# The Fourier branch of a two-layer diffusion trunk: c_x by tokens, the position transform ahead of the channel transform

## The chip, the cores and the metric

The kernel runs on one core of a Trainium2 chip. The metric is the device time of one execution in microseconds; the kernel before takes 1150.8 us (median of 3 runs, 1149.96 to 1150.83). The engines named below are TensorE (PE in the profile, its weight loads PEld), VectorE (DVE), ScalarE (ACT), GpSimd (POOL) and SyncE (SP), which issues most of the DMAs.

## The reference, cut to what matters

Two layers (`DEPTH = 2`) work on 256 latent tokens and 256 context tokens of width 2048. In each layer one projection `h @ w_in` gives the columns of three branches: a gMLP branch (a_u, a_v, a_g), attention (q, k, v, b_g) and the Fourier branch (c_x, c_g), which is

```python
def fourier_mix(xc, w_f, b_f):
    bsz, t, _ = xc.shape
    xg = xc.reshape(bsz, t, C_GROUPS, C_DIM).astype(jnp.float32)
    y = jnp.fft.fft2(xg, axes=(1, 3), norm='ortho').real.astype(xc.dtype)
    y = jnp.einsum('btgc,gcd->btgd', y, w_f) + b_f
    return y.reshape(bsz, t, C_WIDTH)
...
    y_a = chunk_gmlp(jax.nn.gelu(a_u), jax.nn.gelu(a_v), g_sgu, w_s, b_s) * jax.nn.silu(a_g)
    y_b = attn_fn(b_q, b_k, b_v) * jax.nn.silu(b_g)
    y_c = fourier_mix(c_x, w_f, b_f) * jax.nn.silu(c_g)
    return jnp.concatenate([y_a, y_b, y_c], axis=-1)
```

There are four groups of 128 channels; the transform goes over the 256 positions of a stream and the 128 channels of a group, and only its real part is kept. Latent and context tokens are two separate streams. In the last layer only the latent stream needs more than its keys and values. The branches go through an output projection, a norm and a gated residual.

## The kernel before

Matrices are float32 held as two parts, a rounded one and the rest: `split_into` casts on ScalarE (L437) and subtracts on VectorE (L438). A product is three matmuls, `mm3` (L420 to L422), or in layer 1 two, `mm2` (L536, L537), where the rounded and the residual part of the latent activations lie side by side, so that one 512-column and one 256-column matmul do, and `joined` (L542, L543) adds the two halves.

The activations `hh`/`hl` have 16 row tiles (k). Weights come as a stream `W` of halves of 128 x 1024: a DMA into `raw` (3 buffers), the cast `whi` (L398) and the subtraction `wlo` (L400), 4 buffers each, taken by `W.next()` in the order of `units()`. `tunit(n)` computes one head of 128 columns with the weights stationary and the tokens moving: 16 k, 48 matmuls of 512 columns in layer 0; `tunit1` is that of layer 1 with 32 matmuls.

PSUM has two pools: `mm_ps` of six banks and `ms_ps` of two.

TensorE's order is the program's order. Work that depends on other engines is put between its matmuls by `later`: a task is a generator which yields how long its next piece is to lie back, and `later.tick` adds up the time that TensorE was given. VectorE, ScalarE and SP are ordered by a scheduler by priority and readiness.

A layer runs so: a_v and the first a_u heads together (`start_av`, `start_au`; in layer 0 three a_u heads, the third in a bank of the small pool); then the remaining a_u heads (one in layer 0, two in layer 1, phase au); c_x in four units (cx); a_g and c_g in four units each, each with its `gate`; k, v, q, b_g. Tasks:

- `branch_a`: gelus of a_u (L724) and a_v (L726), squares back into the a_v banks (L728), the norm, then four position mixes on TensorE (L736).
- `fourier_mats`: the channel cosine and sine matrices times each group's `w_f` (L751), split into `mg`, `mgl`. It starts 3 us after the phase begins.
- `fourier(g, ps)`, one for each c_x unit as it ends: cosine and sine parts are taken apart by adding and subtracting mirrored positions (L760 to L764), split, multiplied by the folded channel matrices (`ps_f`), split again with a repair of one partition, and after `YF` multiplied by the position matrices `ct` and `nst` (`ps_z`), then copied with the bias (L781).
- in layer 1 `boundary_ctx`, begun by `after_start` at the start of c_x: it closes layer 0 for the context (multiplications, an accumulating DMA from GpSimd, squares), takes a norm (column sums L458 and a broadcast L471 through the small pool) and makes layer 1's context activations (`make_h`, L498 to L507), which the k units read.
- `mods`: the modulation of both layers on VectorE (L204, L206) from 512 KB loads into `mraw`, paced by `W.next()`; in layer 1 the gate (L242, L244) from the k units on.

The constants `ct` and `nst` are loaded as two blocks of 128 x 256 and split. The output rows of the groups lie in `yo[12..15]` in layer 0 and in `kt` buffers in layer 1.

Of the kernel before, what the change touches and what calls it, by code (L numbers as in the profile page):

```python
# [7 lines left out]
F32 = mybir.dt.float32  # L8
F32R = mybir.dt.float32r
BF16 = mybir.dt.bfloat16  # L10
AF = mybir.ActivationFunctionType
ALU = mybir.AluOpType

P = 128
D = 2048
KT = D // P
S = 256
T = 2 * S
# [6 lines left out]
COL = dict(au=0, av=512, ag=1024, q=1536, k=2560, v=2816, bg=3072, cx=4096, cg=4608)  # L25


def units():

    u = []  # L30
    u += [("av", COL["av"], 512, 4 * i, 4) for i in range(4)]
    u += [("au01", COL["au"], 256, 8 * i, 8) for i in range(2)]
    u += [(f"au{h}", COL["au"] + 128 * h, 128, 0, 16) for h in (2, 3)]
    u += [(f"cx{h}", COL["cx"] + 128 * h, 128, 0, 16) for h in range(4)]
    u += [(f"ag{h}", COL["ag"] + 128 * h, 128, 0, 16) for h in range(4)]
    u += [(f"cg{h}", COL["cg"] + 128 * h, 128, 0, 16) for h in range(4)]
    u += [(f"k{h}", COL["k"] + 128 * h, 128, 0, 16) for h in range(2)]
    u += [("v", COL["v"], 256, 8 * i, 8) for i in range(2)]
    u += [(f"q{h}", COL["q"] + 128 * h, 128, 0, 16) for h in range(8)]
    u += [(f"bg{h}", COL["bg"] + 128 * h, 128, 0, 16) for h in range(8)]  # L40
    return u
# [9 lines left out]
COFF, _o = {}, 0  # L51
# [3 lines left out]
NCONST = _o  # L55
# [11 lines left out]
def trunk_kernel(ctx: ExitStack, tc: tile.TileContext, xT, xhalf, cT, wss, wsl, wmod, win, wout0, wout1, const, vec, rows,  # L67
                 wmat, bs, sink, out):
    nc = tc.nc
    V, A, G, PE, DMA = nc.vector, nc.scalar, nc.gpsimd, nc.tensor, nc.sync  # L70
# [6 lines left out]
    def sb(shape, dt, tag, bufs=1):  # L77
        cnt[0] += 1
        return pool.tile(shape, dt, tag=tag, bufs=bufs, name=f"{tag}_{cnt[0]}")

    def w2k(shape, dt=F32):
        return sb(shape, dt, "w2k", W2K)

    def mm_ps(name="mm"):
        cnt[0] += 1
        return psum.tile([P, 512], F32, tag="mm", bufs=6, name=f"ps_{name}_{cnt[0]}")

    def ms_ps(name="ms"):
        cnt[0] += 1
        return psum.tile([P, 512], F32, tag="ms", bufs=2, name=f"ps_{name}_{cnt[0]}")  # L90


    yo = [sb([P, T], F32, f"yo{k}") for k in range(KT)]
    ct = sb([P, KT, 2], F32, "ct")
# [29 lines left out]
    def vc(l, name):  # L124
        o, w = VOFF[name]
        return vecs[:, l, o:o + w]

    identr = sb([P, P], F32R, "identr")
    ident = identr.bitcast(F32)
# [143 lines left out]
    state = {"ctx": [], "phase": "", "owed": 0.0}  # L273
    mods = mod_rest()
    LAG = 400
    YF = [5.0, 2.8], [6.0, 5.2]
    RATE = dict(au0=2, cx0=2.2, ag0=2.2, cg0=2.2, k0=2, v0=2, q0=1.8, bg0=2.2, out0=2.8,
                k1=2.5, v1=2.5, q1=1, bg1=0.3, out1=1.4)
    NEAR = [0] * 14 + [1, 2, 3]
# [46 lines left out]
    later = Later()  # L326
# [90 lines left out]
    W = Stream()  # L417

    def mm3(ps, st, mv, start, stop):
        PE.matmul(ps, st[0], mv[0], start=start, stop=False)  # L420
        PE.matmul(ps, st[0], mv[1], start=False, stop=False)  # L421
        PE.matmul(ps, st[1], mv[0], start=False, stop=stop)  # L422

    def part(w, c):

        def of(t):
            if not isinstance(t, list):
                return t[:, c]
            n = t[0].shape[-1]
            return t[c.start // n][:, c.start % n:c.start % n + c.stop - c.start]  # L430

        return of(w[0]), of(w[1])

    split = {}

    def split_into(hi, lo, src):
        A.copy(hi, src)  # L437
        V.tensor_tensor(out=lo, in0=src, in1=hi.bitcast(F32), op=ALU.subtract)  # L438
        return hi, lo

    def split_of(src, tag):
        n = src.shape[-1]
        return split_into(sb([P, n], F32R, tag + "h"), sb([P, n], F32R, tag + "l"), src)
# [38 lines left out]
    def h_of(l, k, sl):  # L482

        if l == 0:
            return hh[k][:, sl], hl[k][:, sl]
        s, a = sl.start // S, sl.start % S
        t, b = (hh, hl)[s][k], a + sl.stop - sl.start
        return t[:, a:b], t[:, S + a:S + b]
# [30 lines left out]
    FULL, LAT, CTX = slice(0, T), slice(0, S), slice(S, T)  # L519
    PASS = 0.648 / T  # L520

    def tunit(n, sl=None):

        sl = slice(0, n) if sl is None else sl
        ps = mm_ps("t")
        for k in range(KT):
            if k % 8 == 0:
                w = W.next()
            c = slice((k % 8) * P, (k % 8 + 1) * P)
            mm3(ps[:, sl], part(w, c), (hh[k][:, sl], hl[k][:, sl]), k == 0, k == KT - 1)  # L530
            later.tick(PASS * n)
        return ps
# [13 lines left out]
    def tunit1(streams):  # L546

        pss = [mm_ps("t") for _ in streams]
        for k in range(KT):
            if k % 8 == 0:  # L550
                w = W.next()
            for s, ps in zip(streams, pss):
                mm2(ps, part(w, slice((k % 8) * P, (k % 8 + 1) * P)), (hh, hl)[s][k], k)
                later.tick(PASS * S)
        return [joined(ps) for ps in pss]
# [12 lines left out]
    def layer(l):  # L568
        last = l == 1
        n = S if last else T  # L570
        nt = n // P
        ysl = (lambda k: y1[k] if k < 4 else yo[k][:, S:T]) if last else (lambda k: yo[k])
        y1 = {}
        if last:
            a = sb([P, 4, 256], F32, "macc")
# [3 lines left out]
        ytmp = (lambda k: y1.get(k)) if last else ysl  # L579
# [32 lines left out]
        if l == 0:  # L612
            for k in range(KT):
# [21 lines left out]
                if k == 0:  # L635
                    start_av(0, range(nt))
                    take_in(3)
                    e = W.emitting(512)
# [51 lines left out]
                start_av(k0 + 1, range(nt))  # L690
            start_au(k0 + nk - 1)
        if l == 0:
            for k in range(KT):
                yo[k] = sb([P, T], F32, f"yo{k}")

            DMA.dma_start(cst[:, NFIRST - P:], const[:, NFIRST:NKEEP])
            with low(LOWC):
                for name in ("m0", "ct", "nst"):
                    o, w = COFF[name]
                    raw = w2k([P, w])  # L700
                    DMA.dma_start(raw, const[:, o:o + w])
                    if w == P:
                        split[name] = sb([P, P], F32R, f"{name}r")
                        A.copy(split[name], raw)
                    else:
                        split[name] = split_of(raw, f"{name}r")

        ws = sb([P, 4, P], F32, "ws")
        DMA.dma_start(ws, wmat[l, 0])
# [38 lines left out]
        def fourier_mats():  # L748
            for j, nm in enumerate(("cc", "sc")):
                ps = ms_ps("mg")  # L750
                PE.matmul(ps, cc(nm), wf.rearrange("p g d -> p (g d)"), start=True, stop=True)  # L751
                split_into(mg[0][:, :, j], mg[1][:, :, j], ps.rearrange("p (g d) -> p g d", d=P))
            yield 0.0

        def fourier(g, ps):


            e = w2k([P, n // S, 2, P])
            p2 = ps[:, 0:n].rearrange("p (s t) -> p s t", t=S)
            A.copy(e[:, :, :, 0:1], ps[:, 0:n].rearrange("p (s j t) -> p s j t", j=2, t=P)[:, :, :, 0:1])  # L760
            back = w2k([P, n // S, P])
            A.copy(back, p2[:, :, P:S])
            for j, op in enumerate((ALU.add, ALU.subtract)):
                V.tensor_tensor(out=e[:, :, j, 1:P], in0=p2[:, :, 1:P], in1=back[:, :, P - 1:0:-1], op=op)  # L764
            x = split_into(w2k([P, n], F32R), w2k([P, n], F32R), e.rearrange("p s j t -> p (s j t)"))
            yield YF[l][0]
            z = mm_ps("z")
            mgg = [m[:, g].rearrange("p a b -> p (a b)") for m in mg]
            for s in range(n // S):
                a = ms_ps("f1")  # L770
                for j in range(2):
                    t = 2 * s + j
                    mm3(a[:, j * 256:(j + 1) * 256], part(x, slice(t * P, (t + 1) * P)), mgg, True, True)
                a1 = w2k([P, 2, P], F32R), w2k([P, 2, P], F32R)
                split_into(*a1, a.rearrange("p (q d) -> p q d", d=P)[:, 0::3])
                split_into(a1[0][0:1, 1], a1[1][0:1, 1], a[0:1, 256:384])
                yield YF[l][1]
                zs = z[:, s * S:(s + 1) * S]
                for j, nm in enumerate(("ct", "nst")):
                    mm3(zs, [m[:, j] for m in a1], split[nm], j == 0, j == 1)  # L780
            A.activation(ytmp(12 + g), z[:, 0:n], AF.Identity, bias=vc(l, "bf")[:, g:g + 1])  # L781


        def rope(hi, lo, ps, ctx=None):
# [94 lines left out]
            V.scalar_tensor_tensor(out=ysl(k), in0=th, scalar=0.5, in1=ysl(k) if 4 <= k < 12 else ytmp(k), op0=ALU.mult, op1=ALU.mult)  # L879

        later.add(branch_a())
        later.add(fourier_mats(), 3.0)
        later.tick(0.0)
        state["phase"] = f"au{l}"
        for h in range(len(au), 4):
            ps = tunit1([0])[0] if last else tunit(n)
            A.activation(ytmp(h), ps[:, 0:n], AF.Gelu_apprx_tanh)
        after_start(l)
        state["phase"] = f"cx{l}"
        for g in range(4):  # L890
            ps = tunit1([0])[0] if last else tunit(n)
            later.add(fourier(g, ps))
            later.tick(0.0)
        state["phase"] = f"ag{l}"
        for h in range(4):
            ps = tunit1([0])[0] if last else tunit(n)
# [23 lines left out]
                mm3(vps[t][:, 0:256], h_of(l, k, ts), part(w, c), k == 0, k == KT - 1)  # L920
        for t in range(4):
            split_into(*part(vv, slice(t * 256, (t + 1) * 256)), vps[t][:, 0:256])
        state["phase"] = f"q{l}"
        for h in range(8):
            ps = tunit1([0])[0] if last else tunit(n)
# [354 lines left out]
```

## Time and profile before

| | |
|---|---|
| median of the runs | 1150.8 us |
| span of the profiled execution | 1148.5 us |
| TensorE's weight loads, busy | 934.0 us |
| q1 (DMA), share of 16 engines | 61.1% |
| HBM read | 231.08 MB, 203 GB/s over the span |
| granted TensorE clock | 9 (90% or more) in all 40 slices |

The profiled execution is one of its own. Its span goes from the first instruction to the last; the time of a run has 2.3 us (1150.8 less 1148.5) around it. In the profile a group's row gives line, engine, operation, output and inputs, shapes and count, then busy time, mean duration and the idle time before it; a row of the timeline gives start, duration and, in brackets, the idle time and who ended it; a row of the windows gives each engine's busy time in a stretch, with its instructions in brackets. Durations of matmuls overlap, so the distance from start to start is what one costs in a row of them. A few matmul records are missing from the trace.

### The profile page before, as it was taken

The numbers are of one execution on the slowest core, as the hardware profiler recorded it, in microseconds if no ns is written. First come the engines' busy times: TensorE is split into PE (matmuls) and PEld (weight loads), VectorE is DVE, ScalarE is ACT, GpSimd is POOL, SyncE is SP. The second block draws the span as 40 slices with busy tenths as digits, with TensorE's granted clock in tenths as the row PEclk, the third lists the DMA queues.
The fourth block names the chain that finished last, engine by engine and source line by source line (L and its number), as shares of the span: only waits on it lengthen the run. The fifth ranks groups of instructions, "written<-read, shape, count | busy, mean of one in ns | idle before, by whom it ended". The sixth has DMA issues, their size and how long they took to land.

```text
span 1148.5 us, 17015 instructions
## 1 busy us (share of the span) xinstructions
PE 1132.7 (99%) x6387; PEld 934.0 (81%) x6391; DVE 884.7 (77%) x1503; ACT 523.0 (46%) x964; POOL 32.4 (3%) x39
## 2 busy tenths in 40 slices
PE   8999999999999999999999999999999999999997
PEld 3566688888898888888888888888888988888885
DVE  1545479999988787888999994386888689868874
ACT  5322343322234666642523323365664369856541
POOL 0000000000000000000000000200500000000001
PEclk9999999999999999999999999999999999999999
DMA  9999755566666344355556664356956786555972
GB/s 353 403 369 345 257 183 180 169 217 209 203 196 186 109 137 129 101 184 182 184 185 216 220 198 153 102 164 203 220 160 208 217 278 193 171 162 192 310 238 74
DMA packets 72803, 234.30 MB, mean 204 GB/s; under 512 B 8464, under 2 KB 11664, under 8 KB 72720
## 3 DMA queue, kind: packets, MB, share of 16 engines
q1 hardware_dynamic: 70416, 231.11, 61.1%
q0 software_dynamic: 2304, 2.10, 1.2%
q8 instruction: 50, 0.82, 0.3%
q14 instruction: 33, 0.27, 0.1%
HBM read 231.08 MB, written 2.10 MB: 203 GB/s over the span
## 4 chain that ended last, share of the span: by engine, by line
PE 87%; DMA 5%; DVE 4%; issue 2%; ACT 1%; SPq 0%; POOL 0%; DVEq 0%; ACTq 0%; POOLq 0%
PE ps_t L420 15%; PE ps_t L422 15%; PE ps_t L421 15%; PE ps_t L536 10%; PE ps_t L537 5%; PE ps_mod L169 2%; PE ps_av L420 2%; PE ps_av L421 2%; PE ps_av L422 2%; DMA mraw<-in_wmod_dram 2%; DVE wlo L400 2%; PE ps_tp L864 2%; PE ps_v L421 1%; PE ps_v L422 1%; PE ps_v L420 1%
## 5 line engine op out<-in xcount | busy, mean ns | idle before, releaser
L398 ACT CAST whi<-raw 128x1024 fp32r<-128x1024 f32 (+1 forms) x216 | 224.3, 1041 | 333.2 <-PE ps_t L421 224.6
L400 DVE TENSOR_TENSOR wlo<-raw,whi 128x1024 fp32r<-128x1024 f32 (+1 forms) x216 | 260.8, 1210 | 71.9 <-ACT whi L398 69.8
L420 PE MATMUL ps_t<-hh,whi 128*128 128x512 f32 (+1 forms) x768 | 294.2, 383 | 1.0 <-ACT yo L724 1.0
L422 PE MATMUL ps_t<-hh,wlo 128*128 128x512 f32 (+1 forms) x768 | 292.6, 381 | 0.0
L421 PE MATMUL ps_t<-hl,whi 128*128 128x512 f32 (+1 forms) x768 | 292.5, 381 | 0.0
L206 DVE SCALAR_TENSOR_TENSOR macc<-mraw,cs,macc 128x512 f32<-128x512 f32 x360 | 248.9, 744 | 16.3 <-DMA mraw<-in_wmod_dram 16.0
L536 PE MATMUL ps_t<-hh,whi 128*128 128x512 f32 x512 | 185.2, 400 | 0.0
L420 PEld LDWEIGHTS ps_t<-hh,whi 128*128 128x128 f32 x768 | 144.4, 188 | 29.0 <-issue 1.5
L422 PEld LDWEIGHTS ps_t<-hh,wlo 128*128 128x128 f32 x768 | 144.4, 188 | 28.0
L421 PEld LDWEIGHTS ps_t<-hl,whi 128*128 128x128 f32 x768 | 144.4, 188 | 25.9 <-issue 0.2
L537 PE MATMUL ps_t<-hh,wlo 128*128 128x256 f32 x512 | 143.2, 280 | 0.0
L536 PEld LDWEIGHTS ps_t<-hh,whi 128*128 128x128 f32 x512 | 96.2, 188 | 21.2 <-issue 0.2
L537 PEld LDWEIGHTS ps_t<-hh,wlo 128*128 128x128 f32 x512 | 96.6, 189 | 0.2 <-issue 0.2
L502 ACT ACTIVATE hh<-w2k,sh 128x256 fp32r<-128x256 f32 x48 | 21.8, 502 | 82.5 <-DVE w2k L498 82.5
L420 PE MATMUL ps_y<-whi,hh 128*128 128x512 f32 x104 | 41.3, 397 | 0.0
L422 PE MATMUL ps_y<-whi,hh 128*128 128x512 f32 x104 | 40.6, 390 | 0.0
L421 PE MATMUL ps_y<-wlo,hh 128*128 128x512 f32 x104 | 40.5, 390 | 0.0
L420 PE MATMUL ps_av<-whi,hh 128*128 128x512 f32 x96 | 39.7, 413 | 0.6 <-ACT hh L502 0.6
L421 PE MATMUL ps_av<-wlo,hh 128*128 128x512 f32 x96 | 38.0, 396 | 0.4 <-DVE wlo L400 0.4
L437 ACT CAST w2k<-ps_tp 128x512 fp32r<-128x512 f32 x40 | 23.4, 584 | 23.1 <-PE ps_scc L421 12.7
L450 POOL TENSOR_TENSOR rs_b<-rs_a,mhalf 128x2 f32<-128x2 f32 (+1 forms) x7 | 7.5, 1066 | 797.1 <-DVE rs_a L448 797.1
L844 ACT ACTIVATE w2k<-w2k,den 128x512 f32<-128x512 f32 (+1 forms) x48 | 27.8, 643 | 1.8 <-DVE den L840 1.6
(380 smaller groups left out, 1760.4 us busy)
## 6 DMA issues: line engine op xcount, KB each, us to landing
raw<-in_win_dram SPq DMA_DIRECT2D x160, 512.0 KB, 3.8
mraw<-in_wmod_dram SPq DMA_DIRECT2D x128, 512.0 KB, 4.4
raw<-in_wout_dram SPq DMA_DIRECT2D x60, 512.0 KB, 4.5
mraw<-in_wsl_dram SPq DMA_DIRECT2D x16, 512.0 KB, 6.0
yo<-in_xT_dram SPq DMA_DIRECT2D x16, 256.0 KB, 5.4
macc<-in_wsl_dram SPq DMA_DIRECT2D x8, 512.0 KB, 7.3
vv<-in_wsl_dram SPq DMA_DIRECT2D x8, 512.0 KB, 8.1
mg<-in_wsl_dram SPq DMA_DIRECT2D x8, 512.0 KB, 5.5
```

What stands on the lines that cost most here:

```text
L169: PE.matmul(ps[32 * kk:32 * kk + 32, 0:n], cpad[:, kg * 4 + kk], ws[kk], start=kg == 0, stop=kg == 3, tile_position=(0, 32 * kk))
L206: V.scalar_tensor_tensor(out=acc[:, s], in0=w[:, kk % 2], scalar=c, in1=acc[:, s], op0=ALU.mult, op1=ALU.add)
L398: A.copy(ph, rc)
L400: self.last = V.tensor_tensor(out=pl, in0=rc, in1=ph.bitcast(F32), op=ALU.subtract)
L420: PE.matmul(ps, st[0], mv[0], start=start, stop=False)
L421: PE.matmul(ps, st[0], mv[1], start=False, stop=False)
L422: PE.matmul(ps, st[1], mv[0], start=False, stop=stop)
L437: A.copy(hi, src)
L536: PE.matmul(ps, w[0], h, start=k == 0, stop=False)
L537: PE.matmul(ps[:, 0:S], w[1], h[:, 0:S], start=False, stop=k == KT - 1)
L844: A.activation(prob[i][:, b * w:(b + 1) * w], prob[i][:, b * w:(b + 1) * w], AF.Copy, scale=den[:, c:c + 1])
L864: PE.transpose(tp[:, (2 * j + b) * P:(2 * j + b + 1) * P], src, ident)
```

## The change

c_x is computed with the tokens stationary and all 512 columns of the four groups moving, in `positions()`, so that its result has tokens in partitions: four banks in layer 0, two in layer 1. Its weights are laid out in the stream for that (four blocks of four k's). The tiles are split whole (`xs`, kept in `yo4` to `yo11` in layer 0 and in the `mraw` buffers in layer 1), and `fourier(g, xs)` multiplies by the position matrix first, then by the folded channel matrices, for the even part (129 positions, with one column more) and the odd part; sums and differences of the two give the positions and their mirrors. The position matrix is made by four transposes of the loaded table and one split. `fourier_mats` starts 13 us after the phase begins in layer 0, with 3 us between its two matrices; the groups start after c_x, by `YS`, 4 us and then every 8 us in layer 0, 8.5 and every 4.5 us in layer 1. The remaining a_u head of layer 0 takes its bank from the small pool.

```diff
-    u += [(f"cx{h}", COL["cx"] + 128 * h, 128, 0, 16) for h in range(4)]
+    u += [("cx", COL["cx"], 512, 4 * i, 4) for i in range(4)]
...
-    YF = [5.0, 2.8], [6.0, 5.2]
+    YF = 4.0, 3.0
+    YS = [4.0, 8.0], [8.5, 4.5]
+    YM = [(13.0, 3.0), (3.0, 0.0)]
...
-    def tunit(n, sl=None):
+    def tunit(n, sl=None, ps=None):
...
-        ps = mm_ps("t")
+        ps = mm_ps("t") if ps is None else ps
...
+                raw = w2k([P, P])
+                DMA.dma_start(raw, const[:, COFF["m0"][0]:COFF["ct"][0]])
+                split["m0"] = sb([P, P], F32R, "m0r")
+                A.copy(split["m0"], raw)
+                tab = sb([P, 2, 2, P], F32, "nstrh")
+                DMA.dma_start(tab, const[:, COFF["ct"][0]:NCONST].rearrange("p (i j t) -> p i j t", i=2, j=2))
...
                 split_into(mg[0][:, :, j], mg[1][:, :, j], ps.rearrange("p (g d) -> p g d", d=P))
+                yield YM[l][1]
+            if not last:
+                ps = ms_ps("dft")
+                for j in range(2):
+                    for i in range(2):
+                        PE.transpose(ps[:, (2 * j + i) * P:(2 * j + i + 1) * P], tab[:, i, j], ident)
+                split["dft"] = split_into(sb([P, T], F32R, "ctrh"), sb([P, T], F32R, "ctrl"), ps)
             yield 0.0
...
+        def positions():
+
+            cps = [mm_ps("cx") for _ in range(nt)]
+            for k in range(KT):
+                if k % 2 == 0:
+                    w = W.next()
+                for t in range(nt):
+                    mm3(cps[t], h_of(l, k, slice(t * P, (t + 1) * P)),
+                        part(w, slice((k % 2) * 512, (k % 2 + 1) * 512)), k == 0, k == KT - 1)
+                later.tick(PASS * 512 * nt)
+            if last:
+                xh, xl = (sb([P, 2, 512], F32R, "mraw", 2) for _ in range(2))
+                xs = [(xh[:, t], xl[:, t]) for t in range(2)]
+            else:
+                xs = [[sb([P, 512], F32R, f"yo{4 + 2 * t + i}") for i in range(2)] for t in range(4)]
+            for x, ps in zip(xs, cps):
+                split_into(*x, ps)
+            return xs
...
+        def fourier(g, xs):
+
+
+            ns = n // S
+            f1 = ms_ps("f1")
+            for s in range(ns):
                 for j in range(2):
...
+                    mm3(f1[:, s * S:(s + 1) * S], part(xs[2 * s + j], slice(g * P, (g + 1) * P)),
+                        part(split["dft"], slice(j * S, (j + 1) * S)), j == 0, j == 1)
+            a = split_into(w2k([P, ns, S], F32R), w2k([P, ns, S], F32R),
+                           f1[:, 0:n].rearrange("p (s t) -> p s t", t=S))
+            yield YF[l]
+            even, odd = (ps[:, 0:ns * w].rearrange("p (s t) -> p s t", t=w)
+                         for ps, w in ((mm_ps("z"), P + 2), (ms_ps("f2"), P)))
+            mm3(even, [m[:, g, 0] for m in mg], [t[:, :, 0:P + 2] for t in a], True, True)
+            mm3(odd, [m[:, g, 1] for m in mg], [t[:, :, P:S] for t in a], True, True)
+            e = w2k([P, ns, P + 2])
+            A.activation(e, even, AF.Identity, bias=vc(l, "bf")[:, g:g + 1])
+            y = ytmp(12 + g).rearrange("p (s t) -> p s t", t=S)
+            A.copy(y[:, :, 0:P + 1:P], e[:, :, 0:P + 1:P])
+            V.tensor_tensor(out=y[:, :, 1:P], in0=e[:, :, 1:P], in1=odd[:, :, 1:P], op=ALU.add)
+            V.tensor_tensor(out=y[:, :, S - 1:P:-1], in0=e[:, :, 1:P], in1=odd[:, :, 1:P], op=ALU.subtract)
...
         later.add(branch_a())
-        later.add(fourier_mats(), 3.0)
+        later.add(fourier_mats(), YM[l][0])
...
-            ps = tunit1([0])[0] if last else tunit(n)
+            ps = tunit1([0])[0] if last else tunit(n, ps=ms_ps("t"))
...
+        xs = positions()
         for g in range(4):
-            ps = tunit1([0])[0] if last else tunit(n)
-            later.add(fourier(g, ps))
-            later.tick(0.0)
+            later.add(fourier(g, xs), YS[l][0] + g * YS[l][1])
```

Left out are the removed body of the old `fourier`, the old loop over the constants, and the allocation of `yo4` to `yo11`, which moves from the layer's start to the point before q.

More of the change, by code (lines that the diff above doesn't have):

```diff
@@ L692, in layer @@
         if l == 0:
-            for k in range(KT):
+            for k in (0, 1, 2, 3, 12, 13, 14, 15):
                 yo[k] = sb([P, T], F32, f"yo{k}")
@@ L697, in layer @@
             with low(LOWC):
[L698 to L706, printed above, removed]
+                raw = w2k([P, P])
[4 more added lines that the diff above has]
+                DMA.dma_start(tab, const[:, COFF["ct"][0]:NCONST].rearrange("p (i j t) -> p i j t", i=2, j=2))
         ws = sb([P, 4, P], F32, "ws")
@@ L752, in fourier_mats @@
                 split_into(mg[0][:, :, j], mg[1][:, :, j], ps.rearrange("p (g d) -> p g d", d=P))
-            yield 0.0
[L755 to L770, printed above, removed]
-                for j in range(2):
[L772 to L781, printed above, removed]
@@ L922, in layer @@
             split_into(*part(vv, slice(t * 256, (t + 1) * 256)), vps[t][:, 0:256])
+        if not last:
+            for k in range(4, 12):
+                yo[k] = sb([P, T], F32, f"yo{k}")
         state["phase"] = f"q{l}"
```

## The prediction, before the changed kernel ran

> **What bounds the kernel now.** I read the page first, then the chain of waits, then TensorE's list of waits, and at last the timeline of TensorE where the Fourier branch runs.
>
> ```profile
> span 1148.5 us, 17015 instructions
> PE 1132.7 (99%) x6387; PEld 934.0 (81%) x6391; DVE 884.7 (77%) x1503; ACT 523.0 (46%) x964; POOL 32.4 (3%) x39
> PE 87%; DMA 5%; DVE 4%; issue 2%; ACT 1%; SPq 0%; POOL 0%; DVEq 0%; ACTq 0%; POOLq 0%
> PE ps_t L420 <- ACT yo L724: 1.0, 1, 1.0
> PE ps_z L422 <- DVE w2k L438: 0.8, 2, 0.5
> ```
>
> TensorE is busy for 99% of the span and 87% of the chain is its own work. So the time is the sum of what TensorE issues plus its few waits, and the two waits shown (one on the bank of the fourth a_u head, one on a split inside the Fourier groups) are among the longest that it has. A matmul's duration in the profile overlaps its neighbours', so I price matmuls by the distance from one start to the next:
>
> ```profile
> 235.08 0.39 PE L422 MATMUL ps_t<-hh,wlo 128*128 128x512 f32 x1
> ...
> 235.98 0.39 PE L420 MATMUL ps_t<-hh,whi 128*128 128x512 f32 x1
> 777.72 0.39 PE L422 MATMUL ps_av<-whi,hh 128*128 128x512 f32 x1
> ...
> 778.64 0.39 PE L536 MATMUL ps_au<-hh,whi 128*128 128x512 f32 x1
> 820.41 0.39 PE L536 MATMUL ps_t<-hh,whi 128*128 128x512 f32 x1
> 820.64 0.28 PE L537 MATMUL ps_t<-hh,wlo 128*128 128x256 f32 x1
> 820.75 0.39 PE L536 MATMUL ps_t<-hh,whi 128*128 128x512 f32 x1
> 822.14 0.28 PE L420 MATMUL ps_f<-mg,w2k 128*128 128x256 f32 x1
> 822.26 0.27 PE L421 MATMUL ps_f<-mgl,w2k 128*128 128x256 f32 x1
> ```
>
> Both long stretches hold four matmuls: 0.90/4 = 0.225 us for 512 columns into one bank, 0.92/4 = 0.23 us where the bank changes every three matmuls (a_v by tokens). A 512/256 pair of layer 1 takes 0.345 us, a 256-column matmul of the Fourier groups 0.12 us.
>
> **The change part by part.**
>
> *c_x by tokens.* Layer 0: 4 heads x 16 rows x 3 = 192 matmuls of 512 columns before, and 4 token tiles x 16 x 3 = 192 after. Layer 1: 64 pairs before, 64 x 0.345 = 22.1 us; after, 2 tiles x 16 x 3 = 96 matmuls, 96 x 0.23 = 22.1 us. Nothing is saved. In layer 0 the bank now changes every three matmuls: 192 x (0.23 - 0.225) = 1.0 us at most, nothing at least; I take +0.5, since two-decimal starts can't separate the two. Weights are as many bytes in as many halves, each serving as many matmul-microseconds as before, so their loads and splits keep their rhythm.
>
> *Position stage first.* Before, a group had 12 matmuls of 256 columns in the first product and 12 in the second (half of that in layer 1). After, layer 0 has 12 of 256, then 3 of 260 and 3 of 256 columns: 6 fewer in each of four groups, 24 x 0.12 = **-2.9 us**. In layer 1 the count stays at 12 a group; 24 matmuls shrink from 256 to 130 or 128 columns. What those cost, the rows show from both sides:
>
> ```profile
> 396.03 0.22 PE L814 MATMUL ps_sc<-m0r,identr 128*128 128x128 f32 x1
> 396.03 0.19 PEld L420 LDWEIGHTS ps_sc<-kt,w2k 128*128 128x128 f32 x1
> 396.09 0.45 PE L420 MATMUL ps_sc<-kt,w2k 128*128 128x512 f32 x1
> 396.14 0.19 PEld L421 LDWEIGHTS ps_sc<-ws,w2k 128*128 128x128 f32 x1
> 396.37 0.39 PE L421 MATMUL ps_sc<-ws,w2k 128*128 128x512 f32 x1
> 157.65 0.89 PE ps_mix L736 x8
> 379.01 0.44 PE ps_tp L864 x4
> ```
>
> The 128-column mask matmul lets the next start 0.06 us later, but the weight load behind that one starts 0.11 us after the load before it, and the next matmul comes 0.28 instead of 0.23 us later: the 0.06 gained is mostly given back. Where 128-column instructions with loads of their own follow each other (mix, transposes) they stand 0.11 apart. I take 0.11, as the new products also load before each matmul: 24 x 0.01 = -0.2 us; by 0.06 it would be -1.4 us. [...]
>
> The four transposes that make the position matrix, once in layer 0, cost as the transposes in the row: +0.44 us. The folded matrices are computed with the same matmuls, only later.
>
> *The bank of the fourth a_u head.*
>
> ```profile
> 142.59 0.40 PE L422 MATMUL ps_au<-hh,yo 128*128 128x512 f32 x1
> 144.02 0.50 PE L420 MATMUL ps_t<-hh,whi 128*128 128x512 f32 x1 [1.03 <-ACT yo L724]
> 143.37 1.58 ACT L724 ACTIVATE yo<-ps_au 128x512 f32<-128x512 f32 x3
> 150.46 0.68 ACT L728 ACTIVATE ps_av<-w2k 128x512 f32<-128x512 f32 x1
> ```
>
> TensorE stood 144.02 - 142.59 - 0.23 = 1.2 us until ScalarE had emptied an a_u bank. The new bank (of the small pool) held only a modulation result that VectorE had read before, and the order of the built program gives that unit no wait on ScalarE: **-1.2 us**. What is late next is c_x, which wants four large banks at once. It starts at 142.8 + 48 x 0.225 = 153.6, and ScalarE had finished all gelus and squares by 151.1, with other work in between that the new order puts behind them. So it waits for none, with 2.5 us to spare; without that cover it would be the 1.2 us again.
>
> *The splits of c_x* (four in layer 0, two in layer 1) stand before the groups:
>
> ```profile
> L437 ACT CAST w2k<-ps_tp 128x512 fp32r<-128x512 f32 x40 | 23.4, 584 | 23.1 <-PE ps_scc L421 12.7
> ```
>
> Four such casts of 0.58 us, each with a subtraction on VectorE behind it, take some 3 us; the first bank is done 2 us before the last. TensorE runs 21 matmuls (4.7 us) of the next unit before layer 0's first group, and 27 pairs (9.3 us) in layer 1. I count them as hidden; with the cover gone the first group waits for the last cast and subtraction, about 1.2 us.
>
> *The old waits of the groups.*
>
> ```profile
> 823.69 0.28 PE L421 MATMUL ps_z<-nstrl,w2k 128*128 128x256 f32 x1
> 824.47 0.38 PE L422 MATMUL ps_z<-nstrh,w2k 128*128 128x256 f32 x1 [0.50 <-DVE w2k L438]
> ```
>
> Here the one-partition repair of the sine part was late: 0.78 - 0.12 = 0.66 us. The wait list puts 0.3 of its 0.8 on a second such place, which with the same hidden part makes some 0.45. Both go with the repair: **-1.1 us**.
>
> *New waits.* In layer 1 the built order gives the first product of groups 1 and 2 a wait on VectorE that groups 0 and 3 don't have: the small pool has two banks, and the chain of the context's norm (its column sums, then its broadcast) takes a bank in between, so these two must wait until the adds of the group before have read its odd bank. Those adds stand behind a weight split and a gate:
>
> ```profile
> 836.51 1.05 ACT L398 CAST whi<-raw 128x1024 fp32r<-128x1024 f32 x1 [1.11 <-PE ps_t L536]
> 839.56 0.42 ACT L877 ACTIVATE w2k<-join 128x256 f32<-128x256 f32 x1 [1.73 <-DVE join L543]
> 837.97 1.23 DVE L400 TENSOR_TENSOR wlo<-raw,whi 128x1024 fp32r<-128x1024 f32 x1
> 839.11 0.41 DVE L543 TENSOR_TENSOR join<-join,ps_t 128x256 f32<-128x256 f32 x1
> 840.01 0.43 DVE L878 SCALAR_TENSOR_TENSOR w2k<-w2k,join 128x256 f32<-128x256 f32 x1 [0.48 <-ACT w2k L877]
> 840.69 0.41 DVE L879 SCALAR_TENSOR_TENSOR macc<-w2k,macc 128x256 f32<-128x256 f32 x1
> ```
>
> From the cast, which starts as a unit ends, to the end of the gate are 841.1 - 836.5 = 4.6 us here, 4.2 without the 0.4 in which the subtraction waited after the cast; the group's two adds lengthen it by up to 0.5: 4.2 to 4.7. TensorE gets from the unit's end to group 1's first product in 10 matmuls, 6 short ones, 8 matmuls and the column sums: 1.7 + 0.7 + 1.4 + 0.3 = 4.1 us; to group 2's in 6, 6 short, 6, the broadcast and 2: 1.0 + 0.7 + 1.0 + 0.3 + 0.3 = 3.3. The waits are 0.1 to 0.6 and 0.9 to 1.4; I take **+1.5 us** together. Whether more is late in VectorE's queue is the rival below.
>
> *The rest.* The column sums of the context move 46 matmuls later against the gate units (some 8 us), since layer 1's ticks are four times as coarse in the token loop. Its last columns were ready well before use:
>
> ```profile
> 848.00:879.00 31.00, 31.00 (x181) 27.14 (x180) 29.85 (x57) 20.61 (x36) 0.00 (x0) 1.00 0.61 186
> 873.94 0.48 DVE L507 SCALAR_TENSOR_TENSOR hl<-w2k,sh,hl 128x256 fp32r<-128x256 f32 x1
> L536 PE MATMUL ps_t<-hl,whi x32: 392/392/392, 879.0 to 900.4; 128*128 128x512 f32 x32
> mraw<-in_wmod_dram SPq DMA_DIRECT2D x128, 512.0 KB, 4.4
> ```
>
> The last is read 11 row pairs into the first k unit, at 879.0 + 11 x 0.69 = 886.6; 874.4 + 8 leaves 4 us. On SP's queue one constant load replaces two. In layer 1 c_x's splits lie in the modulation buffers, so the gate's first two loads go to the queue some 40 places later, in the second c_g unit; they land in 4.4 us and are wanted two units (11 us) on. Cost nothing; late, they would hold VectorE with the weight splits behind.
>
> **Sum:** -2.9 - 0.2 + 0.4 + 0.5 - 1.2 - 1.1 + 1.5 = -3.0 us. The profiled span of 1148.5 becomes 1145.5; the runs' median of 1150.8 is 2.3 above that span, so I predict **1147.8 us**.
>
> **The rivals.**
>
> 1. *No new waits* (12%): the adds come in time, since the old chain carried work that is gone. -4.5, 1146.3 us. For it: in the built order VectorE has 1188 rows instead of 1210 and ScalarE 772 instead of 803. Against it: the six rows above.
> 2. *Narrow matmuls stream* (7%): 0.06 us each in layer 1, 1.2 us more, 1146.6. Against it are the load distance and the mix row.
> 3. *The change doesn't do all it says* (13%): a wait stays at the fourth head's unit or at c_x's start, because a bank is not empty, and the token loop costs its full 1.0 us: -3.0 + 1.2 + 0.5 = -1.3, 1149.5 us, within 0.2%.
> 4. *VectorE's queue, slower* (18%): in layer 1 the second products now follow 20 matmuls (3.45 us) after the first, not 32 (5.5 us). If a group's split is as late as before, ready 5.5 + 0.66 and 5.5 + 0.45 after, the waits are 2.7 and 2.5, and for the two groups that had none anything to 2.05, 1 each in the middle: 7.2 us in all in place of the 1.5. -4.5 + 7.2 = +2.7, 1153.5 us. It is slower than before from 1.1 us a group on, and by over 0.2% from 1.7. For it: VectorE is busy 29.85 of 31 us in the window row. Against it: the built order runs the groups after most of the context's multiplications and squares, and there is no repair behind the split.
>
> **How the numbers follow.** The forecast has 50%, with its own range from 1146.3 to 1149.4 (the bounds of the new waits and of the bank changes); some 8 of these points lie within 0.2%, which is 2.3 us and about what a measurement of this kernel can tell from no change. Faster: 42 + 12 + 7 = 61%. Same: 8 + 13 = 21%. Slower: 18%. All gains at their bounds give -2.9 - 1.4 + 0.4 - 1.2 - 1.1 = -6.2, 1144.6, the fourth rival 1153.5 and more; leaving out a tenth on each side makes 1145.2 to 1153.2.
>
> **What would show it.** In the new profile: 18 Fourier matmuls a group in layer 0, 0.12 apart; no wait before the fourth a_u head; starts 0.11 apart in layer 1's even and odd products (0.06 for rival 2); one wait on VectorE before the first product of groups 1 and 2 there, of 0.3 and 1.2 us. Waits before the even products of layer 1 would mean rival 4, a wait on ScalarE at the first c_x matmul rival 3, and a wait in the k units that the context's columns came late after all. Wrong would be the whole frame if TensorE stood idle elsewhere in the span for more than it did.

## The result, and the profile after

| | before | after |
|---|---|---|
| median of the runs (21 each) | 1151.33 us | 1153.14 us |
| lowest and highest | 1149.87 to 1153.33 | 1151.41 to 1155.20 |
| span of the profiled execution | 1148.5 us | 1152.7 us |
| granted TensorE clock, mean of that execution | 0.998 | 0.995 |

The changed kernel is slower by 0.2%: the ratio is 1.0017, with a 95% interval of 1.0011 to 1.0024. The prediction said 1147.8 us, faster by 3.0. The profiled executions lie 4.2 us apart and the medians 1.8, because the one of after took 1154.5 us from end to end (1.4 above its median), 1.8 of them outside the span, while before's 1148.5 with the same 1.8 would make 1150.3 (1.0 below its median). I account for the 4.2 below, since that is what the trace can show.

First the changed kernel's page, with the lines that answer those shown of before:

```profile
span 1152.7 us, 16855 instructions
PE 1133.4 (98%) x6335; PEld 932.4 (81%) x6339; DVE 880.2 (76%) x1480; ACT 515.8 (45%) x933; POOL 31.8 (3%) x39
```

TensorE has 52 instructions fewer (6335 instead of 6387), yet it is "busy" 0.7 us longer in a span 4.2 us longer. A busy time that grows while the count falls is a first sign that some matmuls ran slowly. TensorE's list of waits of after says what else is new (what is waited for; total, times, longest):

```profile
PE ps_t L538 <- ACT whi L400: 2.4, 2, 2.1
PE ps_t L539 <- DVE wlo L402: 1.4, 2, 0.8
```

The fourth a_u head's wait on `yo` is gone. Two waits on a weight (`whi` from ScalarE, `wlo` from VectorE) stand at and near the head of the list instead.

Where along the span the time went, the timeline of TensorE tells by the same milestones in both kernels. Before, at the first matmul of layer 1's a_v, of layer 1's v, and of the first output product:

```profile
753.62 0.39 PE L420 MATMUL ps_av<-whi,hh 128*128 128x512 f32 x1
...
900.79 0.28 PE L420 MATMUL ps_v<-whi,hh 128*128 128x256 f32 x1
...
1045.82 0.40 PE L420 MATMUL ps_y<-whi,hh 128*128 128x512 f32 x1
```

After, the same view with the same three rows, and more that the later sections use:

```profile
142.78 0.39 PE L424 MATMUL ps_au<-hh,yo 128*128 128x512 f32 x1
143.01 0.39 PE L422 MATMUL ps_t<-hh,whi 128*128 128x512 f32 x1
...
208.12 0.28 PE L422 MATMUL ps_f<-ctrh,yo 128*128 128x256 f32 x1
...
209.43 0.28 PE L424 MATMUL ps_f<-ctrh,yo 128*128 128x256 f32 x1
214.35 0.28 PE L422 MATMUL ps_z<-w2k,mg 128*128 128x260 f32 x1
...
214.94 0.28 PE L424 MATMUL ps_f<-w2k,mgl 128*128 128x256 f32 x1
...
749.55 0.39 PE L422 MATMUL ps_av<-whi,hh 128*128 128x512 f32 x1
...
824.13 0.28 PE L539 MATMUL ps_t<-hh,wlo 128*128 128x256 f32 x1
824.72 0.49 PE L538 MATMUL ps_t<-hh,whi 128*128 128x512 f32 x1 [0.31 <-ACT whi L400]
825.98 0.39 PE L539 MATMUL ps_t<-hh,wlo 128*128 128x256 f32 x1 [0.76 <-DVE wlo L402]
...
828.55 0.28 PE L539 MATMUL ps_t<-hh,wlo 128*128 128x256 f32 x1
830.93 0.63 PE L538 MATMUL ps_t<-hh,whi 128*128 128x512 f32 x1 [2.11 <-ACT whi L400]
832.19 0.58 PE L539 MATMUL ps_t<-hh,wlo 128*128 128x256 f32 x1 [0.63 <-DVE wlo L402]
832.57 0.63 PE L538 MATMUL ps_t<-hh,whi 128*128 128x512 f32 x1
...
837.69 0.53 PE L538 MATMUL ps_t<-hh,whi 128*128 128x512 f32 x1
838.07 0.28 PE L539 MATMUL ps_t<-hh,wlo 128*128 128x256 f32 x1
...
845.58 0.36 PE L422 MATMUL ps_f<-ctrh,mraw 128*128 128x256 f32 x1
...
853.29 0.35 PE L422 MATMUL ps_f<-ctrh,mraw 128*128 128x256 f32 x1 [0.79 <-DVE kt L801]
...
864.15 0.33 PE L423 MATMUL ps_z<-w2k,mg 128*128 128x130 f32 x1 [0.44 <-DVE w2k L440]
864.32 0.27 PE L424 MATMUL ps_z<-w2k,mgl 128*128 128x130 f32 x1
864.43 0.28 PE L422 MATMUL ps_f<-w2k,mg 128*128 128x128 f32 x1
...
905.09 0.28 PE L422 MATMUL ps_v<-whi,hh 128*128 128x256 f32 x1
...
1050.08 0.40 PE L422 MATMUL ps_y<-whi,hh 128*128 128x512 f32 x1
```

When layer 1 begins, the changed kernel is 753.62 - 749.55 = 4.1 us ahead. From there to v it takes 155.5 us instead of 147.2, 8.4 more, and from v to the first output product nothing changes (145.0 us in both). So what lies ahead of layer 1 won 4.1 us, somewhat more than the 3.2 that the prediction's terms for it add up to (-2.9 + 0.4 + 0.5 - 1.2), and one stretch of layer 1 gave back twice that.

In that stretch the rows show three losses.

- *Weights late.* Measured from start to start, less what the matmul costs without a wait (0.12 after a 256-column one, 0.23 after a 512-column one), the four waits are 0.47, 1.03, 2.26 and 1.03: 4.8 us.
- *A slow clock.* From 832.57 to 837.69 stand eight 512/256 pairs, 0.64 us apart where they cost 0.345: 8 x 0.295 = 2.4 us, and some 0.4 more at the two edges (832.19 to 832.57, 837.69 to 838.07). The view of stretches, whose number after the engines is the granted clock, says the same, and by it the 0.50 lasts from 831.2 to 837.9 us:

```profile
832.50:838.00 5.50, 5.50 (x18) 4.73 (x18) 5.47 (x9) 3.64 (x5) 0.00 (x0) 0.50 0.61 182
```

- *Waits of the groups.* The first product of group 1 starts 0.3 us late (845.58), that of group 2 0.95 (853.29), and one even product waits 0.6 (864.15): 1.8 us.

Together that is 4.8 + 2.8 + 1.8 = 9.4. Less the old waits (1.1) and the narrower products (0.2) it makes 8.1 of the 8.4; 0.3 stays unexplained.

*Why the weights were late.* The timeline of ScalarE in after, just before and within the gaps:

```profile
807.48 1.05 ACT L400 CAST whi<-raw 128x1024 fp32r<-128x1024 f32 x1 [2.34 <-issue]
811.37 0.42 ACT L1143 ACTIVATE acc<-yo 128x256 f32<-128x256 f32 x1 [2.84 <-DMA yo<-in_xhalf_dram]
812.04 0.42 ACT L1143 ACTIVATE w2k<-yo 128x256 f32<-128x256 f32 x1 [0.26 <-DMA yo<-in_xhalf_dram]
815.69 0.42 ACT L1143 ACTIVATE w2k<-yo 128x256 f32<-128x256 f32 x1 [3.23 <-DMA yo<-in_xhalf_dram]
816.02 1.03 ACT L400 CAST whi<-raw 128x1024 fp32r<-128x1024 f32 x1
...
823.31 0.42 ACT L1143 ACTIVATE w2k<-yo 128x256 f32<-128x256 f32 x1 [2.74 <-DMA yo<-in_xhalf_dram]
823.63 1.03 ACT L400 CAST whi<-raw 128x1024 fp32r<-128x1024 f32 x1
...
829.53 0.42 ACT L1143 ACTIVATE w2k<-yo 128x256 f32<-128x256 f32 x1 [1.45 <-DMA yo<-in_xhalf_dram]
829.85 1.03 ACT L400 CAST whi<-raw 128x1024 fp32r<-128x1024 f32 x1
```

Line 1143 is `boundary_ctx`'s square of the context columns of one `yo`; it can start only when GpSimd's accumulating DMA of that column block has landed. From the cast at 816.02 on, two to four squares stand ahead of each weight cast up to 829.85. None of these casts has a wait of its own in brackets: each starts 0.32 or 0.33 us after the start of the square before it. So 8.5 us pass between the casts at 807.48 and 816.02, and for 6.3 of them ScalarE stood idle. Before, the same engine did this:

```profile
811.88 0.42 ACT L1121 ACTIVATE acc<-yo 128x256 f32<-128x256 f32 x1 [2.21 <-DMA yo<-in_xhalf_dram]
...
812.48 1.04 ACT L398 CAST whi<-raw 128x1024 fp32r<-128x1024 f32 x1
...
813.74 0.41 ACT L1121 ACTIVATE w2k<-yo 128x256 f32<-128x256 f32 x1
...
815.15 1.05 ACT L398 CAST whi<-raw 128x1024 fp32r<-128x1024 f32 x1
816.10 0.42 ACT L1121 ACTIVATE w2k<-yo 128x256 f32<-128x256 f32 x1
816.75 0.42 ACT L1121 ACTIVATE w2k<-yo 128x256 f32<-128x256 f32 x1 [0.23 <-DVE macc L742]
...
819.32 1.05 ACT L398 CAST whi<-raw 128x1024 fp32r<-128x1024 f32 x1
...
823.30 1.64 ACT L1121 ACTIVATE w2k<-yo 128x256 f32<-128x256 f32 x5
```

One or two squares stood ahead of a cast, with the copies and splits of the old groups in between, and the casts came every 2.6 to 4.2 us. The first run of five squares came only at 823.30, and found its transfers landed.

In the changed kernel the waiting closes into a ring, by the timeline of VectorE in after:

```profile
817.08 1.23 DVE L402 TENSOR_TENSOR wlo<-raw,whi 128x1024 fp32r<-128x1024 f32 x1 [4.16 <-ACT whi L400]
818.22 0.42 DVE L1138 TENSOR_TENSOR yo<-yo,rbs 128x256 f32<-128x256 f32 x1
```

The subtraction waits for the cast; behind it stand the multiplications (L1138) whose results the next accumulating DMAs carry; and for these DMAs the next squares wait, with the next cast behind them. The view of the squares' line sums it up, after and then before:

```profile
  DMA yo<-in_xhalf_dram: 11.6, 9
  DVE yo L1138: 2.7, 1
```

```profile
  DMA yo<-in_xhalf_dram: 2.8, 2
```

In after ScalarE sat idle ahead of the 16 squares for 14.3 us (11.6 + 2.7); before it was 2.8 for the transfers. It is busy for only 45% of the span, and still it holds TensorE up.

### The profile page after: what moved, and what is told of

Same layout as the page of the kernel before. It is cut to its first block, busy times and chain, and to the rows that moved or that the text cites. A ratio compares the mean times of both kernels' runs of the same rounds, so it can differ in the third digit from the quotient of the medians.

```text
span 1152.7 us, 16855 instructions
## 1 busy us (share of the span) xinstructions
PE 1133.4 (98%) x6335; PEld 932.4 (81%) x6339; DVE 880.2 (76%) x1480; ACT 515.8 (45%) x933; POOL 31.8 (3%) x39
## 4 chain that ended last, share of the span: by engine, by line
PE 87%; DMA 5%; DVE 4%; issue 1%; ACT 1%; POOL 1%; SPq 0%; DVEq 0%; ACTq 0%; POOLq 0%
PE ps_t L422 14%; PE ps_t L424 13%; PE ps_t L423 13%; PE ps_t L538 9%; PE ps_t L539 5%; PE ps_mod L169 2%; PE ps_av L422 2%; PE ps_av L424 2%; PE ps_av L423 2%; DVE wlo L402 2%; DMA mraw<-in_wmod_dram 2%; PE ps_tp L884 2%; PE ps_cx L422 1%; PE ps_cx L424 1%; PE ps_cx L423 1%
## 5 line engine op out<-in xcount | busy, mean ns | idle before, releaser
L422 PE MATMUL ps_t<-hh,whi 128*128 128x512 f32 (+1 forms) x704 | 268.2, 381 | 0.0
L424 PE MATMUL ps_t<-hh,wlo 128*128 128x512 f32 (+1 forms) x704 | 267.6, 380 | 0.0
L423 PE MATMUL ps_t<-hl,whi 128*128 128x512 f32 (+1 forms) x704 | 267.4, 380 | 0.0
L538 PE MATMUL ps_t<-hh,whi 128*128 128x512 f32 x448 | 166.4, 407 | 2.4 <-ACT whi L400 2.4
L424 PEld LDWEIGHTS ps_t<-hh,wlo 128*128 128x128 f32 x704 | 132.4, 188 | 25.2
L422 PEld LDWEIGHTS ps_t<-hh,whi 128*128 128x128 f32 x704 | 132.4, 188 | 24.9 <-issue 1.2
L423 PEld LDWEIGHTS ps_t<-hl,whi 128*128 128x128 f32 x704 | 132.4, 188 | 23.7
L539 PE MATMUL ps_t<-hh,wlo 128*128 128x256 f32 x448 | 127.2, 284 | 1.4 <-DVE wlo L402 1.4
L538 PEld LDWEIGHTS ps_t<-hh,whi 128*128 128x128 f32 x448 | 85.5, 191 | 22.4 <-ACT whi L400 3.1
L539 PEld LDWEIGHTS ps_t<-hh,wlo 128*128 128x128 f32 x448 | 86.0, 192 | 2.9 <-DVE wlo L402 2.4
L422 PE MATMUL ps_cx<-whi,hh 128*128 128x512 f32 x96 | 38.9, 405 | 0.0
L423 PE MATMUL ps_cx<-wlo,hh 128*128 128x512 f32 x96 | 37.4, 389 | 0.0
```

What stands on the lines that cost most here:

```text
L538: PE.matmul(ps, w[0], h, start=k == 0, stop=False)
L539: PE.matmul(ps[:, 0:S], w[1], h[:, 0:S], start=False, stop=k == KT - 1)
```

## The experiments

The theory before the first of them: the squares' places in ScalarE's queue cost layer 1 the weights and with them the clock. Its rivals: the token loop in layer 1 itself is slow (or its coarse ticks, or the bank shared with the context's norm).

**The squares held behind a later cast.** On ScalarE each square is held behind the weight cast that is the newest when the square is written into the program. The edit touches nothing else.

```diff
-                    A.copy(ph, rc)
+                    self.cast = A.copy(ph, rc)
...
-                A.activation(q, yo[i][:, CTX], AF.Square)
+                with tc.issue_after(W.cast.ins):
+                    A.activation(q, yo[i][:, CTX], AF.Square)
```

> The changed kernel, with each of layer 1's squares of the context columns held on ScalarE behind the weight cast issued last, so that no more than two squares stand between two casts. Theory (squares wait for the accumulating DMAs and hold the weight casts behind them): the four weight waits of TensorE between 824 and 833 us (4.8 us) and the stretch of half clock behind them (some 1.7 us) go: 5 to 7 us less than the changed kernel's 1153.1, 1146 to 1148. Rival (the weight loads themselves come late, because the accumulating DMAs share the DMA engines): the waits stay where the loads land, 1152 to 1154.

Measured: 1146.47 us (1145.69 to 1147.19, 5 runs), before on the same chip 1151.07, ratio 0.9959 with an interval of 0.9947 to 0.9972. That is 6.7 below the changed kernel's median. The timeline of ScalarE in this kernel, and the stretch that covers the old gaps:

```profile
807.82 1.05 ACT L400 CAST whi<-raw 128x1024 fp32r<-128x1024 f32 x1 [2.33 <-issue]
811.02 1.05 ACT L400 CAST whi<-raw 128x1024 fp32r<-128x1024 f32 x1 [2.15 <-PE ps_cx L424]
811.97 0.41 ACT L1144 ACTIVATE acc<-yo 128x256 f32<-128x256 f32 x1
```

```profile
815.00:838.00 23.00, 23.00 (x131) 19.93 (x129) 19.01 (x33) 14.43 (x29) 6.61 (x8) 1.00 0.98 258
```

The second cast comes 3.2 us after the first, before the first square, and waits only for its own buffer (for c_x's matmuls to have read it). TensorE is busy for all of the 23 us, at full clock. None of the four waits on a weight is left, and the slow stretch is gone with them, though nothing was done for the clock. The DMA engines did not become freer: their share (the number behind the clock) is 0.98 over that stretch at 258 GB/s, and 0.83 at 185 GB/s over the same stretch of the changed kernel. So it was the order on ScalarE, and not a load on the DMA engines, that made the weights late. The group waits are still there, and the first has grown from 0.3: 1.3, 0.94 and 0.60 us from start to start.

**Layer 0 alone.** Layer 1 keeps the old units, the old group and its tables; layer 0 is as changed. Shown are only the lines that choose between the two; those that bring the old parts back are left out.

```diff
-        xs = positions()
+        xs = None if last else positions()
...
-            later.add(fourier(g, xs), YS[l][0] + g * YS[l][1])
+            if last:
+                ps = tunit1([0])[0]
+                later.add(fourier_old(g, ps))
+                later.tick(0.0)
+            else:
+                later.add(fourier(g, xs), YS[l][0] + g * YS[l][1])
```

> The change in layer 0 alone; layer 1 has the old units, the old groups and the order of the kernel before on ScalarE and VectorE. Theory: layer 0 gains the 4.1 us that TensorE is ahead at layer 1's first a_v matmuls, and layer 1 costs what it did: about 1147.2. Rival (the loss comes from the modulation or the transfers that layer 0 shifts, and only shows in layer 1): no better than 1151.

Measured: 1146.58 us (1145.90 to 1146.75, 5 runs), ratio 0.9959 (0.9947 to 0.9972), span 1145.0. Layer 0's part alone is worth 4.5 us against before on the same chip (1151.07), and layer 1's part, as it came, costs 6.6. The two kernels together say that the loss sits in layer 1 and is not the token loop itself: with the squares held, the whole kernel is as fast as this one (1146.47 and 1146.58), and from a_v to v layer 1 takes 148.2 us there and 147.9 here.

**The head's bank alone.** The kernel before, with the fourth head's bank from the small pool and the matrices 10 us later in layer 0.

```diff
-        later.add(fourier_mats(), 3.0)
+        later.add(fourier_mats(), 3.0 if last else 13.0)
...
-            ps = tunit1([0])[0] if last else tunit(n)
+            ps = tunit1([0])[0] if last else tunit(n, ps=ms_ps("t"))
```

> The kernel before, with only the fourth a_u head's bank from the small pool and the folded matrices 13 us after the phase begins in layer 0. Theory: the 1.2 us of waiting for ScalarE go, 1150.1 against 1151.3. Rival (the small pool's banks are then missing for the mixes and the folded matrices): 1151 or more, with a new wait at a mix or at a folded matrix.

Measured: 1151.61 us (1150.38 to 1152.51, 11 runs), ratio 1.0002 (0.9993 to 1.0011): no change. The head's wait is gone, and a row of this kernel's TensorE timeline shows what took its place:

```profile
161.65 1.13 PE L751 MATMUL ps_mg<-w2k,cst 128*128 128x512 f32 x2 [1.45 <-DVE w2k L738]
```

The second matrix needs the small bank of a position mix, until VectorE has read it (L738). A wait of 1.2 us was traded for one of 1.45. The change has 3 us between its two matrices, and its trace shows no such wait.

**The same with the matrices apart.** To the kernel just told, layer 0's second matrix comes 3 us behind the first.

```diff
+                if not last:
+                    yield 3.0
```

> The kernel before, with the fourth a_u head's bank from the small pool and, in layer 0, the folded matrices 13 us after the phase begins and 3 us apart. Theory: the 1.4 us wait at the second folded matrix came from the two standing together, with a mix's bank still unread; apart, it goes, and the head's wait stays gone: 1.2 us less than before, 1149.9. Rival (the small pool is short by a bank with three users): as before, 1151.1, with a wait at a mix or a folded matrix.

Measured: 1150.61 us (1148.55 to 1152.73, 11 runs) beside 1150.98 of before; ratio 0.9998 (0.9989 to 1.0007). In the profile (span 1147.3) both waits are gone. But the times do not resolve the 1.2 us: 1149.9 was expected, and the profiled execution (1149.06) was a fast one of the eleven. That the wait goes is shown by the trace; what it is worth in time is not shown.

**Another bank for layer 1's odd product.** It is taken from the six large banks, so that the first product of the next group shares none with it.

```diff
-                         for ps, w in ((mm_ps("z"), P + 2), (ms_ps("f2"), P)))
+                         for ps, w in ((mm_ps("z"), P + 2), ((mm_ps if last else ms_ps)("f2"), P)))
```

> The changed kernel, with layer 1's odd products in the large pool. Theory: the waits of the first products of groups 1 and 2 on VectorE (0.26 and 0.95 us) go and nothing else changes, 1151.9 against 1153.1. Rival (VectorE is behind anyway, and the next product that needs it waits instead): 1153, with the wait at an even product or in the k units.

Measured: 1149.78 us (1148.46 to 1150.72, 11 runs), ratio 0.9987 (0.9978 to 0.9995), 3.4 below the changed kernel and so 2 better than expected. TensorE's list of waits has neither `ps_f` nor `ps_z` any more, but still the weights:

```profile
PE ps_t L538 <- ACT whi L400: 2.4, 1, 2.4
PE ps_t L539 <- DVE wlo L402: 1.3, 2, 0.8
```

In the profiled executions layer 1 from a_v to v takes 151.6 us, 3.9 less than in the changed kernel. The group waits make 1.8 of that. The slow stretch was shorter in this execution, five pairs at 0.64 instead of eight, 3 x 0.295 = 0.9 us less, and the waits for weights were 0.4 shorter; 0.8 stays open. Nothing in these rows ties the last three to the bank. Why the median, too, fell by 1.6 more than the group waits isn't shown: the mean clocks of the 11 runs, 0.995 to 0.999, spread as those of the changed kernel do.

**Finer ticks in the token loop.** Each 512-column step gives its own tick, so that tasks come between c_x's matmuls as finely as before.

```diff
-                later.tick(PASS * 512 * nt)
+                    later.tick(PASS * 512)
```

> The changed kernel, with layer 1's and layer 0's ticks after each token tile instead of after all tiles of a row. In the built order ScalarE then has six squares (the fifth to the tenth) between two weight casts. Theory (squares ahead of casts starve TensorE, whatever the ticks): weight waits stay, in one place, with 2 us or more: 1150 to 1154. Rival (the coarse ticks were the cause, since they delay the context's chain): the waits go, 1146 to 1148.

Measured: 1151.95 us (1150.64 to 1153.91, 10 runs), ratio 1.0012 (1.0002 to 1.0021). The waits for weights stay: 1.08, 1.03, 0.32 and 1.13 us from start to start, 3.6 in all. The coarse ticks aren't the cause of these. The expected single wait of 2 us or more did not come, and in this execution the clock did not fall (1.00 from 815 to 842 us). Even products now wait at four places instead of one, two of them in layer 0, for 2.5 us by the list of waits.

**The squares held and the odd bank moved**, the two edits above together.

> Both edits: squares held behind the weight casts, and layer 1's odd products in the large pool. Theory: what is left of layer 1's loss are the waits of the first products of groups 1 and 2 (1.3 and 0.9 us with held squares) and of the last even product (0.6), so 2.2 to 2.8 us less than with held squares alone: 1143.7 to 1144.3, against 1151.1 before. Rival (VectorE is behind and the wait moves): 1146.5.

Measured: 1145.49 us (1143.39 to 1145.59, 5 runs), before 1150.98, ratio 0.9947 (0.9935 to 0.9960), span 1143.7. The median came 1.2 us above the upper end of what was expected; the two fastest runs, 1143.39 and 1143.83, do not lie above it. In the profile TensorE's list has no wait left between 780 and 890 us, and from a_v to v layer 1 takes 145.4 us; but layer 0's first stage, ahead of every edited place, ran late in it: the wait of the a_u heads on a cast is 1.0 us there and 0.3 in the changed kernel, and layer 1 begins at 751.77 instead of 749.55.

**All three: squares, bank and ticks.**

> Held squares, odd products in the large pool and ticks after each token tile. Theory: no weight wait, no bank wait; the context's chain is earlier by some us, which matters only where VectorE is late: 1143.5 to 1144.3, the same as with the first two. Rival (finer ticks bring the context's work back among the groups): 1145 to 1147 with waits at even products.

Measured: 1145.15 us (1144.72 to 1145.41, 5 runs), ratio 0.9950 (0.9937 to 0.9962). That is above the expected 1143.5 to 1144.3 and inside the rival's range, and the rival's sign is there: one even product waits 0.8 us (from 854.62 to 855.49). The median is the same as without the finer ticks, but the ticks gain nothing: from a_v to v layer 1 takes 147.0 us here, and 145.4 without them. Either of the two kernels is about 0.5% faster than before and 0.7% faster than the change as it was made.

## Why the prediction was wrong

The step that failed is a term put at nothing. Under *c_x by tokens* the prediction says of the weights that "their loads and splits keep their rhythm", because as many bytes serve as much matmul time as before, and "The rest" sets no price on it. The bytes are as said, but the casts lost their rhythm: two of them came 8.5 us apart, TensorE waited 4.8 us for weights, and 2.8 more went at half clock (granted 0.50). "The rest" looked at whether the context's columns would be ready in time and whether the modulation loads would land, and not at what the change moves *within* ScalarE's queue. The prediction even used that order: it counted ScalarE's rows (772 instead of 803) as a sign for fewer waits, and against the fourth rival it held that "the built order runs the groups after most of the context's multiplications and squares". That was true, and it was the danger: the old Fourier groups' copies and splits had stood among the squares, with one, one, two and one square ahead of successive casts and only then five together. In the new order the squares stand ahead of the casts by three, four, two and three, before their transfers have landed. The last sentence of the prediction named the consequence without a cause: the frame is wrong "if TensorE stood idle elsewhere in the span". It did, for these 4.8 us.

Why the scheduler moved the squares up (a freer ScalarE, or fewer users of the small buffers that the squares write) was not tried.

The other steps, one by one:

- *Position stage first, layer 0*: right. Twelve matmuls 0.12 apart (208.12 to 209.43), then three and three (214.35 to 214.94): 18 a group. From the fourth head (144.02 before, 143.01 after) to layer 0's v (325.06, 320.96) the time falls from 181.0 to 178.0 us, by 3.1, where -2.9 was said for the groups, +0.44 for the transposes and +0.5 for c_x. The c_x matmuls stand 0.227 us apart, as those of the heads before do, so the +0.5 was not needed.
- *The fourth head's bank*: right as a wait (142.78 to 143.01 is 0.23, no wait). What it is worth in time was not resolved. With the two folded matrices together it only moves the wait to them; the change keeps this wait away by the 3 us between them, which the prediction, with "only later", did not weigh.
- *Narrow products in layer 1*: right at 0.11 (864.32 and 864.43). The rival of 0.06 falls. Their weight loads, too, stand 0.11 apart: five from 864.15 to 864.59.
- *New waits of groups 1 and 2*: right in place and size, 0.3 and 0.95 us where 0.1 to 0.6 and 0.9 to 1.4 were said. The bank experiment shows the mechanism: with another bank both are gone.
- *Old waits of the groups*: gone, as said; one even product of layer 1 waits 0.6 in their place, which only rival 4 had foreseen.
- *The fourth rival*, VectorE's queue, gave 1153.5 us, close to the 1153.14 that came (as a change +2.7, where +1.8 came). Its mechanism is not what happened: it put 7.2 us on the splits inside the groups, and these cost 0.6. The time was right by chance.

With the squares back between the casts, the change is worth -4.6 us in the medians and -3.1 in the spans; -3.0 had been predicted. That the spans agree so well is in part luck: ahead of layer 1 the gain is 3.7 us where the terms make 3.2, layer 1 from a_v to v costs 1.05 where they make 0.2, and the profiled execution was the slowest of its five.

## What to carry to other kernels

When a change takes work out of an engine that is far from busy, compare the order of what is left on that engine, instruction by instruction, and look for one that waits on a slow producer (here an accumulating DMA, a median of 7.3 us from issue to landing) and now stands ahead of one that feeds the bound engine. Here a ScalarE busy for 45% of the span left TensorE waiting for 4.8 us. Where a scheduler decides that order, tie the work whose result is not wanted soon (here the squares) behind the work that the bound engine needs next.

## What the runs showed of the hardware

- *ScalarE kept the order of its queue in these rows.* The cast at 816.02 came behind a square that waited 3.23 us for a DMA; with the squares held the same cast ran at 811.02.
- *A short shortage of work cost twice here: 4.8 us of waits, and 2.8 us lost at a lower clock behind them.* In the changed kernel the clock was granted at 0.50 from 831.2 to 837.9 us, after idle stretches of which none was longer than 2.3 us, and TensorE had work for most of that time. From 828.55 to 832.19, 3.64 us, TensorE started one matmul, at 830.93, and the clock fell right behind it (1.00 up to 831, 0.50 from 831.2), before the second wait was over. With the bank moved, after waits of 2.6 and 1.0 us, it was 0.57 over the 4 us from 832; with finer ticks, after 1.1 and 1.0 us, it stayed at 1.00 in the profiled execution. What made it fall in the one execution and not in the other, these runs do not show.
- *The clock differed from execution to execution.* Over the 21 runs of the changed kernel the mean granted clock was between 0.995 and 0.999; the 8 with 0.998 or more have a median of 1152.5 us, the other 13 one of 1153.5. Before had 0.997 or 0.998 in all the runs beside the experiments. So part of the loss seems to be paid only in some executions, the profiled one among them (0.995), which would put it above its median.
